# Weight tiles of 4,352 bytes, filler tiles and two moved helpers in a one-core decoder layer: where the operands of TensorE's products start in SBUF

## The chip, the cores and the metric

The kernel runs on one core of a Trainium2 chip, alone, as one program in one launch. The metric is the time of that program on the device in microseconds (us), the median of three runs.

## What is computed

A hybrid decoder layer in float32 for one sequence of 1,024 tokens with 1,024 features: two token mixers side by side (a gated linear recurrence, HGRN2, with four heads, and a forgetting attention, FoX, with eight), merged by gates, then a SwiGLU feed forward of 2,816 hidden features and a gated per-layer input of 256 features.

```
h = rms_norm(x);  z = h @ w_in                       # 1024 -> 5640 columns
y_a = hgrn2(z);   y_b = forgetting_attention(z)
merged = sigmoid(z_a) * (y_a @ w_branch_a) + sigmoid(z_b) * (y_b @ w_branch_b)
x = x + merged @ w_out
hf = rms_norm(x); x = x + (silu(hf @ w_ffn_gate) * (hf @ w_ffn_up)) @ w_ffn_down
hp = rms_norm(x); x = x + sigmoid(hp @ w_ple_gate) * (p @ w_ple_proj)
```

## The kernel before

Everything is kept transposed where it can be, features on the 128 partitions and tokens along the row. A product to float32 accuracy is made of three in the type float32r: each operand is split into a high and a low part, and `mm3` (lines 147 to 151) adds high by high, high by low and low by high in one PSUM bank. In each of these a 128 by 128 piece of weights is the stationary operand (512 bytes on a partition), and half of the tokens, 512 columns of 4 bytes (2,048 bytes on a partition), is the moving operand.

By its loops the program makes 5,688 such products of 512 columns outside the attention's own score and value products:

- the eight products of V for either mixer (`v_products`, lines 239 to 241, where tokens are stationary and weights move): 384;
- projections of z by 128 columns, eight for the heads of HGRN2 and sixteen for the gates: 24 units of 48, that is 1,152;
- branches, output projection and the gate of the per-layer input, 8 units of 48 each: 1,152; the small product with `p`: 96;
- the feed forward's gate and up, 22 tiles of seven half-size blocks (Winograd's form of Strassen's method) with 12 products each: 1,848;
- the way back, lines 1253 to 1256, 44 steps with 24 products each: 1,056.

The attention's score and value products have 287 more with 512 columns. `nproj` (lines 379 to 402) makes six pairs of units with tokens stationary and 256 columns of weights moving: 960 products of 256 columns, and 192 of 264 in the pair that carries the forget gates too.

TensorE's instructions stand in the order in which the code writes them (a manual schedule). The splits are made by ScalarE (`whi`, line 122) and VectorE (`wlo`, line 123) up to two units ahead, from a raw tile that SyncE's queue loads.

What matters for the change is where tiles start in a partition of SBUF. Pools are laid one behind the other: `const`, `xpool`, `wpool` and the later pools `gp`, `xb`, `ap`, `bp`, `dp`, `dq` from the low end, and pools with `side="right"` (`zpool`, `hg`, `fx`, `tp`, `xq`, `op`, `x1p`) from the high end. All sizes in the pools of operands are multiples of 256 bytes but for one: the tiles `raw`, `whi` and `wlo` of `wpool` hold 4 x 264 = 1,056 columns, that is 4,224 bytes or 16.5 times 256. `const` holds small tiles of many sizes.

```
def wide(tag, dt, bufs=None):
    return wpool.tile([P, 4 * 264], dt, tag=tag, bufs=bufs, name=tag)

cm = const.tile([P, 7 * P + 2 * P], U8, name="cm")     # masks of HGRN2
uh = const.tile([16, P], R, tag="uh", name="uh")       # largest scores, two parts
```

So the built program has these starts, as remainders by 256 bytes:

| tiles | start, bytes | remainder |
|---|---|---|
| `xpool`: x, its parts `xhi` and `xlo`, half of the feed forward's operands `xo` | 25,440 + n x 2,048 | 96 |
| `whi`, three buffers | 99,424 / 103,648 / 107,872 | 96 / 224 / 96 |
| `wlo`, three buffers | 112,096 / 116,320 / 120,544 | 224 / 96 / 224 |
| `gp`, `xb`, `ap` (`sahi`, `salo`, `sbhi`, `sblo`), `dp` (`dhi`, `dlo`), `dq` | | 96 |
| right side: `hg`, `fx` (attention), `xq` (ten of the feed forward's operands), `zpool` | | 224 |

The three buffers of `whi` and of `wlo` are taken in turn, so a unit of weights has its high part at 96 and its low part at 224, or the other way round in one unit of three. Slices of 128 or 256 columns are multiples of 256 bytes further on; the slices of 264 columns (1,056 bytes) step by 32 bytes in the remainder.

Of the kernel before, what the change touches and what calls it, by code (L numbers as in the profile page):

```python
# [9 lines left out]
F32 = mybir.dt.float32  # L10
R = mybir.dt.float32r
U8 = mybir.dt.uint8
# [5 lines left out]
DRAM = bass.MemoryType.DRAM  # L18

P = 128  # L20
# [9 lines left out]
NEG = -1.0e30  # L30
LEVELS = (64, 32, 16, 8, 4, 2, 1)
# [3 lines left out]
# weight units, each [128, 1024], in the order in which they are stored  # L35
# [11 lines left out]
# columns of the packed float32 constants  # L47
# [3 lines left out]
# gate tiles made among the products of the mixers: those that go to DRAM (how many before a unit  # L51
# of z, and after all of them), then those that stay on chip
# [8 lines left out]
def layer(ctx, tc, xT, pT, wts, wf_in, consts, masks, outT):  # L61
# [9 lines left out]
    const = ctx.enter_context(tc.tile_pool(name="const", bufs=1))  # L71
    xpool = ctx.enter_context(tc.tile_pool(name="xpool", bufs=32))
# [12 lines left out]
    cm = const.tile([P, 7 * P + 2 * P], U8, name="cm")  # L85
# [10 lines left out]
    def wide(tag, dt, bufs=None):  # L96
        return wpool.tile([P, 4 * 264], dt, tag=tag, bufs=bufs, name=tag)

    def fetch(u):
        if u not in raws:  # L100
            t = wide("raw", F32, 2)
            raws[u] = t[:, 0:D]
            if u in (16, 17):
                # with the columns of the forget gates
                raws[u] = t
                v = t.rearrange("p (k c) -> p k c", c=264)
                dma(v[:, :, 0:256], wts[u].rearrange("p (k c) -> p k c", c=256))
                dma(v[:, :, 256:264],
                    wf_in.rearrange("p (k c) -> p k c", c=8)[:, (u - 16) * 4:(u - 15) * 4])
            else:  # L110
                dma(raws[u], wts[u])
# [35 lines left out]
    def mm3(ps, w, x, k, first, last):  # L147
        """ps += w[k].T @ x[k] to float32 accuracy, from two-part operands"""
        mm(ps, w[0], x[0], start=first, stop=False)  # L149
        mm(ps, w[0], x[1], start=False, stop=False)  # L150
        mm(ps, w[1], x[0], start=False, stop=last)  # L151
# [10 lines left out]
    def split_scaled(src, gain, h):  # L162
        """two float32r parts of src * gain, one half of the tokens"""
        hi = xpool.tile([P, HALF], R, tag="x", name="xhi")
        lo = xpool.tile([P, HALF], R, tag="x", name="xlo")
        act(hi, src, AF.Copy if gain is None else AF.Identity,  # L166
            scale=1.0 if gain is None else gain)
        if gain is None:
            tt(lo, src, hi.bitcast(F32), ALU.subtract)  # L169
        else:  # L170
            stt(lo, src, gain, hi.bitcast(F32), ALU.mult, ALU.subtract)  # L171
        return hi, lo
# [7 lines left out]
    def rms_stats(acc, bank, tag="r8"):  # L180
        """1 / sqrt(mean + eps) over the features, tokens on the partitions"""
        ps = bank()
        for b in range(8):
            mm(ps[:, b:b + 1], acc[:, b * P:(b + 1) * P], ones1, start=True, stop=True)  # L184
        nat = const.tile([P, 8], F32, tag="nat", name="nat")
        r8 = const.tile([P, 8], F32, tag=tag, name="r8")
        nc.vector.tensor_scalar(nat, ps[:, 0:8], 1.0 / D, EPS, ALU.mult, ALU.add)
        ptt(r8, nat, neghalf[:, 0:8], ALU.pow)
        return r8

    def rms_spread(r8, bank):
        """the same on every partition, tokens along the row"""
        rb = const.tile([P, T], F32, tag="rb", name="rb")
        for h in range(2):
            pr = bank()
            broadcast_rows(r8, h, pr)
            nc.scalar.copy(rb[:, h * HALF:(h + 1) * HALF], pr)  # L197
        return rb
# [3 lines left out]
    # ================= input norm, first products =================  # L202
# [8 lines left out]
    w2 = lambda: hg.tile([P, HALF], F32, tag="w2", bufs=NW, name="w2")  # L211

# [3 lines left out]
    def skew(t, off, *dims):  # L216
        """a view of a tile with free dimensions of given steps and sizes"""
        return bass.AP(t.tensor, t.offset + off, [list(t.ap[0])] + [list(d) for d in dims])

    # V of all heads is made in its natural layout, tokens on the partitions. HGRN2 takes its odd  # L220
    # chunks with the tokens in reverse, which makes room for two chunks in one product.
# [73 lines left out]
    # lower bounds of the forget gate: softmax over the two rows of logits  # L295
# [16 lines left out]
    def zproj(u, dst=None):  # L312
        """one 128-column tile of z, transposed: dst[h] = psum * rb; yields between the products"""
        hi, lo = weight(u)
        if dst is None:
            z = zpool.tile([P, T], F32, tag="z", name="z")
            dst = [hv(z, 0), hv(z, 1)]
        else:
            z = None
        for h in range(2):  # L320
            ps = zbank()
            for k in range(KT):
                s = slice(k * P, (k + 1) * P)
                mm3(ps, (hi[:, s], lo[:, s]), hT[h][k], k, k == 0, k == KT - 1)
                run_deferred()
                if k == KT - 1:
                    tt(dst[h], ps, hv(rb, h), ALU.mult)
                yield
        return z

    # a stream of projections that is worked off between the products of the mixers
# [31 lines left out]
    # ================= HGRN2 =================  # L363
    # K and its decays hold the even chunks first, then the odd ones in reverse
# [14 lines left out]
    def nproj(u, n=256):  # L379
        """columns of z with the tokens on the partitions; yields the chunks that are done"""  # L380
# [22 lines left out]
    def hg_project_gate(g):  # L403
        """g of two heads, tokens on the partitions"""
        Gp = [page("G"), page("G")]
        gain.append([t.rearrange("p (c n d) -> p c n d", n=2, d=P) for t in Gp])
        for done in nproj(12 + 2 * g):
            for c, ps in done:
                act(Gp[c // 4][:, c % 4 * 256:c % 4 * 256 + 256], ps, AF.Identity,
                    scale=rx8[:, c:c + 1])  # L410
            yield

    def hg_decay(h, Fp, Qp, b):
        """forget gate, its log summed over each chunk, and silu of q"""
# [4 lines left out]
        # small gates are scaled into the range of Ln  # L419
# [10 lines left out]
        # K = 1 - forget gate, and the summed log in the order of K  # L430
# [16 lines left out]
    def hg_mix(rate, h, K, bK, Fp, Qp, b):  # L447
# [54 lines left out]
        # between the chunks  # L502
# [97 lines left out]
    def fox_gates(fl):  # L600
        """minus the running sum of the log forget gates, eight heads on eight partitions"""
# [25 lines left out]
    def fox_project(g, i, half):  # L627
        """q or k of four heads, normalised, tokens on the partitions"""
# [50 lines left out]
    # the first two tiles of z; the row of 1 / rms is worked out meanwhile  # L679
# [33 lines left out]
    # V of the attention, in two parts  # L713
# [30 lines left out]
    # ================= forgetting attention =================  # L744
# [24 lines left out]
    def fox_norm(pr, i):  # L769
        """the heads in two parts, tokens along the row; the low part replaces the tile"""  # L770
# [13 lines left out]
    def fox_place(pr):  # L784
        """the operands of the score products of two heads"""
# [25 lines left out]
    def fox_mix(pr, steps, before):  # L811
# [3 lines left out]
        # the largest score of each token (its constant cancels in the softmax)  # L815
# [23 lines left out]
        uh = const.tile([16, P], R, tag="uh", name="uh")  # L839
        ul = const.tile([16, P], R, tag="ul", name="ul")  # L840
# [112 lines left out]
    # ================= gates, branches =================  # L953
# [61 lines left out]
    # ================= output projection, residual =================  # L1015
    # The gate and up products of the feed forward are made by Winograd's form of Strassen's
    # method: seven products of half-size blocks for eight. Blocks: tiles k and k + 4 of the
    # features by the two halves of the tokens (b11 and b21 are the first half of the tokens).
# [18 lines left out]
    def split_to(src, gain, hi, lo):  # L1037
        """two float32r parts of src * gain"""
# [66 lines left out]
    # ================= feed forward, hidden features =================  # L1105
# [8 lines left out]
    def ffn_weights(f):  # L1114
        """operands a11 | a12, a22, s1 | s2, s3 | s4 of one tile of gate and up"""
# [9 lines left out]
        # ru becomes s3 | s1 and rg becomes s2 | s4  # L1125
# [11 lines left out]
    def block(n, w, x):  # L1137
        """one product of half-size blocks"""
# [45 lines left out]
    # ================= feed forward, back to the model's features =================  # L1184
# [79 lines left out]
    # ================= per-layer input =================  # L1264
# [22 lines left out]
    # the products of the first two tiles go on while the row of 1 / rms is worked out  # L1287
# [21 lines left out]
def _tiles(w):  # L1309
    """[1024, n * 128] -> one [128, 1024] unit for each 128 columns"""  # L1310
# [67 lines left out]
```

## Time and profile before

| | |
|---|---|
| median of 3 runs | 1682.18 us (1681.9 to 1684.22) |
| span of the profiled execution, first to last instruction | 1680.8 us, 1.4 us under the median |
| TensorE matmuls (PE) | 1657.3 us busy, 99% of the span, 8,218 instructions |
| weight loads (PEld) | 1376.8 us |
| VectorE (DVE) / ScalarE (ACT) / GpSimd (POOL) | 1041.1 / 634.4 / 456.5 us |
| mean granted TensorE clock | 0.998 |
| DMA | 185.94 MB, mean 111 GB/s |

The duration that the trace gives for a matmul (0.39 us for one of 512 columns) reaches from its start to its end through a pipeline in which the next one has long begun. What a matmul costs in a dense stretch is the time from its start to the start of the next, called its **step** from here on: it is read from the column of start times in the timeline.

### The profile page before, as it was taken

What the parts mean: (1) busy time and instruction counts of PE and PEld (TensorE: products, weight loads), DVE (VectorE), ACT (ScalarE), POOL (GpSimd) and SP (SyncE); (2) the same over time, 40 slices, a digit from 0 to 9 for tenths busy, and PEclk for the clock granted to TensorE, in tenths of its full rate; (3) what the DMA queues carried; (4) which work ended last, traced back from release to release, by engine and by line L of the source; (5) the groups of instructions that cost most, each with busy time, mean ns of one, the idle gap of its engine ahead of it and who ended that gap; (6) DMA issues with size and microseconds to landing.
All of it is one profiled execution on the core that took longest, in us unless ns stands there. A gap on an engine that the chain in (4) does not pass through costs nothing. (4 is left out here: it accounts for less than half of the span.)

```text
span 1680.8 us, 21333 instructions
## 1 busy us (share of the span) xinstructions
PE 1657.3 (99%) x8218; PEld 1376.8 (82%) x8218; DVE 1041.1 (62%) x1466; ACT 634.4 (38%) x943; POOL 456.5 (27%) x364
## 2 busy tenths in 40 slices
PE   8999999999999999999999999999999999999998
PEld 6889889999787777778787888888888788788887
DVE  8457677755666686655577776666776542643532
ACT  7244555642423134552334232333233342543310
POOL 2342444431312021122134344344343000200300
PEclk9999999999999999999999999999999999999999
DMA  5323121236264642351433222222221763354011
GB/s 207 100 87 102 63 76 39 76 115 177 90 150 122 174 103 86 128 195 48 150 138 101 75 87 94 83 76 76 76 88 63 245 225 113 119 200 138 33 68 38
DMA packets 93685, 185.94 MB, mean 111 GB/s; under 512 B 11376, under 2 KB 40432, under 8 KB 93584
## 3 DMA queue, kind: packets, MB, share of 16 engines
q1 hardware_dynamic: 93584, 184.59, 33.9%
q8 instruction: 64, 1.05, 0.3%
q14 instruction: 37, 0.30, 0.1%
HBM read 130.95 MB, written 40.96 MB: 102 GB/s over the span
## 5 line engine op out<-in xcount | busy, mean ns | idle before, releaser
L149 PE MATMUL ps_z<-xhi,whi 128*128 128x512 f32 x630 | 256.5, 407 | 0.1
L150 PE MATMUL ps_z<-xlo,whi 128*128 128x512 f32 x630 | 249.5, 396 | 1.1 <-DVE xlo L169 0.9
L151 PE MATMUL ps_z<-xhi,wlo 128*128 128x512 f32 x630 | 249.5, 396 | 0.0
L149 PEld LDWEIGHTS ps_z<-xhi,whi 128*128 128x128 f32 x630 | 120.6, 191 | 24.2 <-ACT xhi L166 1.2
L150 PEld LDWEIGHTS ps_z<-xlo,whi 128*128 128x128 f32 x630 | 119.0, 189 | 25.8 <-DVE xlo L169 2.4
L151 PEld LDWEIGHTS ps_z<-xhi,wlo 128*128 128x128 f32 x630 | 118.5, 188 | 26.1
L122 ACT CAST whi<-raw 128x1024 fp32r<-128x1024 f32 (+1 forms) x69 | 72.2, 1047 | 166.9 <-PE ps_z L150 128.8
L123 DVE TENSOR_TENSOR wlo<-raw,whi 128x1024 fp32r<-128x1024 f32 (+1 forms) x69 | 98.8, 1432 | 34.7 <-ACT whi L122 23.6
L169 DVE TENSOR_TENSOR xlo<-raw,xhi 128x512 fp32r<-128x512 f32 x88 | 58.7, 688 | 92.5 <-ACT xhi L166 85.8
L394 PE MATMUL ps_z<-whi,xhi 128*128 128x256 f32 (+1 forms) x384 | 112.1, 292 | 0.0
L395 PE MATMUL ps_z<-wlo,xhi 128*128 128x256 f32 (+1 forms) x384 | 108.2, 282 | 0.0
L396 PE MATMUL ps_z<-whi,xlo 128*128 128x256 f32 (+1 forms) x384 | 108.0, 281 | 0.0
L882 POOL TENSOR_SCALAR ph<-p 128x512 fp32r<-128x512 f32 (+3 forms) x96 | 53.5, 562 | 170.6 <-ACT p L878 170.2
L1173 POOL TENSOR_TENSOR w<-w,rb 128x512 f32<-128x512 f32 x44 | 62.9, 1429 | 113.7 <-ACT w L1172 113.7
L166 ACT ACTIVATE xhi<-raw 128x512 fp32r<-128x512 f32 x88 | 53.0, 627 | 104.5 <-PE ps_m L150 59.3
L883 DVE TENSOR_TENSOR pl<-p,ph 128x512 fp32r<-128x512 f32 (+3 forms) x96 | 55.9, 590 | 49.5 <-POOL ph L882 49.1
L1199 POOL TENSOR_TENSOR acc<-acc,sq 128x512 f32<-128x512 f32 x14 | 22.2, 1619 | 229.0 <-issue 118.3
L395 PEld LDWEIGHTS ps_z<-wlo,xhi 128*128 128x128 f32 x384 | 72.4, 189 | 0.8 <-DVE wlo L123 0.2
L394 PEld LDWEIGHTS ps_z<-whi,xhi 128*128 128x128 f32 x384 | 72.7, 189 | 0.1
L878 ACT ACTIVATE p<-ps_m 128x512 f32<-128x512 f32 (+3 forms) x96 | 46.1, 491 | 70.5 <-PE ps_m L874 45.8
L1126 POOL TENSOR_TENSOR ru<-ru 128x512 f32<-128x512 f32 x22 | 36.1, 1642 | 133.7 <-DVE wlo L1041 133.7
L396 PEld LDWEIGHTS ps_z<-whi,xlo 128*128 128x128 f32 x384 | 72.3, 188 | 0.0
(465 smaller groups left out, 4394.1 us busy)
## 6 DMA issues: line engine op xcount, KB each, us to landing
raw<-wts SPq DMA_DIRECT2D x71, 512.0 KB
raw<-hid SPq DMA_DIRECT2D x44, 512.0 KB
rg<-wts SPq DMA_DIRECT2D x22, 512.0 KB
ru<-wts SPq DMA_DIRECT2D x22, 512.0 KB
hid<-w SPq DMA_DIRECT2D x44, 256.0 KB
dr<-wts SPq DMA_DIRECT2D x42, 256.0 KB
gd<-gst SPq DMA_DIRECT2D x24, 256.0 KB
g<-gd SPq DMA_DIRECT2D x24, 256.0 KB
```

Of the source, the lines that this page charges most:

```text
L122: nc.scalar.copy(hi, raw)
L123: tt(lo, raw, hi.bitcast(F32), ALU.subtract)
L149: mm(ps, w[0], x[0], start=first, stop=False)
L150: mm(ps, w[0], x[1], start=False, stop=False)
L151: mm(ps, w[1], x[0], start=False, stop=last)
L169: tt(lo, src, hi.bitcast(F32), ALU.subtract)
L394: mm(ps[:, off:off + n], xh[:, cs], hi, start=k == 0, stop=False)
L395: mm(ps[:, off:off + n], xh[:, cs], lo, start=False, stop=False)
L396: mm(ps[:, off:off + n], xl[:, cs], hi, start=False, stop=k == KT - 1)
L882: pts(ph[:, 0:n], p[:, 0:n], 1.0, 0.0, ALU.mult, ALU.add)
L883: tt(pl[:, 0:n], p[:, 0:n], fb(ph[:, 0:n]), ALU.subtract)
L1173: ptt(s, s, hv(rb, h), ALU.mult)
```

## The change

`WIDE` is 17 x 64 = 1,088 columns, so a tile of `wpool` has 4,352 bytes, 17 times 256. A filler tile of 288 bytes in `const` and one of 480 bytes in a new pool on the right side move the ends of those pools to multiples of 256. The masks `cm` (1,152 bytes) leave `const` for the pool of HGRN2, with 12 x 128 = 1,536 bytes, and the two parts of the largest scores, `uh` and `ul` (512 bytes each), leave it for the attention's pool. Comments go too.

```diff
+WIDE = 17 * 64
+PAD = 72
...
     const = ctx.enter_context(tc.tile_pool(name="const", bufs=1))
+
+    const.tile([P, PAD], F32, name="pad")
+    edge = ctx.enter_context(tc.tile_pool(name="edge", bufs=1, side="right"))
+    edge.tile([P, 120], F32, name="edge")
     xpool = ctx.enter_context(tc.tile_pool(name="xpool", bufs=32))
...
-    cm = const.tile([P, 7 * P + 2 * P], U8, name="cm")
...
     def wide(tag, dt, bufs=None):
-        return wpool.tile([P, 4 * 264], dt, tag=tag, bufs=bufs, name=tag)
+        return wpool.tile([P, WIDE], dt, tag=tag, bufs=bufs, name=tag)
...
-                raws[u] = t
-                v = t.rearrange("p (k c) -> p k c", c=264)
+                raws[u] = t[:, 0:4 * 264]
+                v = raws[u].rearrange("p (k c) -> p k c", c=264)
...
+    cm = hg.tile([P, 12 * P], U8, tag="cm", bufs=1, name="cm")
...
-        uh = const.tile([16, P], R, tag="uh", name="uh")
-        ul = const.tile([16, P], R, tag="ul", name="ul")
+        uh = fx.tile([16, P], R, tag="uh", bufs=1, name="uh")
+        ul = fx.tile([16, P], R, tag="ul", bufs=1, name="ul")
```

In the program that is built, every tile of every pool but `const` starts at a multiple of 256 bytes: `xpool` at 23,552, `raw` at 89,088, `whi` at 97,792, `wlo` at 110,848, and so on. What still starts elsewhere is `const` (the identity, 128 before, now 160; small tiles) and three of each four slices of 264 columns. On every engine the instructions are the same and stand in the same order, with the same sizes and the same transfers; the instructions that compute differ in their addresses alone.

## Rows read from the trace of the kernel before

**Rows 1.** The page, parts 1 and 2: span, busy time, granted clock by slice.

```profile
span 1680.8 us, 21333 instructions
PE 1657.3 (99%) x8218; PEld 1376.8 (82%) x8218; DVE 1041.1 (62%) x1466; ACT 634.4 (38%) x943; POOL 456.5 (27%) x364
PEclk9999999999999999999999999999999999999999
```

**Rows 2.** Waits of PE: engine, line waited for, us in total, times, longest.

```profile
PE ps_z L239 <- ACT xhi L166: 5.6, 1, 5.6
PE ps_a L861 <- DVE pl L883: 2.2, 4, 0.8
...
PE ps_z L150 <- DVE xlo L171: 0.2, 1, 0.2
```

**Rows 3.** Timeline of PE at the first products: start us, duration us, what.

```profile
6.59 0.63 PE L241 MATMUL ps_z<-whi,xlo 128*128 128x512 f32 x1
...
7.87 0.63 PE L241 MATMUL ps_z<-whi,xlo 128*128 128x512 f32 x1
```

**Rows 4.** Stretch 6 to 8 us: us, PE busy (x), PEclk, DMA share, GB/s.

```profile
6.00:8.00 2.00, 2.00 (x6) 1.00 1.00 378
```

**Rows 5.** Timeline of PE on the way back: 49 matmuls, first and last.

```profile
1399.63 0.39 PE L151 MATMUL ps_z<-xhi,dlo 128*128 128x512 f32 x1
...
1410.51 0.39 PE L151 MATMUL ps_z<-xhi,dlo 128*128 128x512 f32 x1
```

**Rows 6.** Timeline of PE, per-layer gate: 43 matmuls of a unit, 45 of the next.

```profile
1594.23 0.40 PE L151 MATMUL ps_z<-xhi,wlo 128*128 128x512 f32 x1
...
1604.03 0.39 PE L151 MATMUL ps_z<-xhi,wlo 128*128 128x512 f32 x1
...
1607.67 0.39 PE L149 MATMUL ps_z<-xhi,whi 128*128 128x512 f32 x1
...
1617.84 0.40 PE L151 MATMUL ps_z<-xhi,wlo 128*128 128x512 f32 x1
```

**Rows 7.** Timeline of PE, feed forward: 47 matmuls, first and last.

```profile
999.63 0.40 PE L151 MATMUL ps_m<-xo,sblo 128*128 128x512 f32 x1
...
1010.27 0.39 PE L149 MATMUL ps_m<-xo,sahi 128*128 128x512 f32 x1
```

**Rows 8.** Timeline of PE, feed forward: third triples of two blocks, from 957.72 and 1018.58.

```profile
957.72 0.40 PE L149 MATMUL ps_z<-xo,sbhi 128*128 128x512 f32 x1
...
958.41 0.39 PE L149 MATMUL ps_z<-xo,sbhi 128*128 128x512 f32 x1
...
1017.90 0.39 PE L149 MATMUL ps_z<-xo,sbhi 128*128 128x512 f32 x1
...
1018.58 0.40 PE L149 MATMUL ps_z<-xo,sbhi 128*128 128x512 f32 x1
...
1019.28 0.39 PE L149 MATMUL ps_z<-xo,sbhi 128*128 128x512 f32 x1
```

**Rows 9.** Timeline of PE among the attention's projections: 128x128 products, then 9 matmuls of 256 columns.

```profile
341.38 1.13 PE L495 MATMUL ps_m<-Q,K 128*128 128x128 f32 x8
342.26 0.36 PE L394 MATMUL ps_z<-whi,xhi 128*128 128x256 f32 x1
342.46 0.28 PE L395 MATMUL ps_z<-wlo,xhi 128*128 128x256 f32 x1
...
343.41 0.28 PE L394 MATMUL ps_z<-whi,xhi 128*128 128x256 f32 x1
```

**Rows 10.** Timeline of PE, pair with the forget gates: slices of 264 columns.

```profile
309.01 0.28 PE L394 MATMUL ps_z<-whi,xhi 128*128 128x264 f32 x1
...
310.10 0.28 PE L394 MATMUL ps_z<-whi,xhi 128*128 128x264 f32 x1
310.22 0.28 PE L395 MATMUL ps_z<-wlo,xhi 128*128 128x264 f32 x1
```

## The prediction

> **What bounds the kernel now.** I read the page first, then TensorE's waits, then start times in the timeline. The page shows PE busy for 99% of the span and no slice of its clock row under the top digit, while VectorE, the next engine, stands at 62% [rows 1]. The waits that stop PE are twelve rows that fall from 5.6 us, once at the start, to 0.2 us [rows 2]; no stage is held up by a split or a transfer for long. So the time is the number of products times their step, and the question is what a step is.
>
> A product of 512 columns has a floor that the trace shows. The first products step by (7.87 - 6.59) / 3 = 0.427 us [rows 3], which is 512 columns at 1.2 GHz, the lower level of the clock (the clock column reads 1.00 there all the same [rows 4]); at this pace each column costs one tick and nothing is added, although these operands lie at remainders 96 and 224 too. At 2.4 GHz the same 512 ticks are half of that, 213.3 ns. No dense stretch reaches it:
>
> - On the way back all operands lie at remainder 96. There 48 steps take 10.88 us, 226.7 ns each [rows 5].
> - In the gate of the per-layer input the moving operand lies at 96. The unit with its high part at 224 and its low part at 96 takes 9.80 us for 42 steps, 233.3 ns; the next, with the high part at 96 and the low at 224, 10.17 us for 44 steps, 231.1 ns [rows 6].
> - In the feed forward, where some moving operands lie at 224 (the ten tiles of `xq`) and the weights of three blocks in seven come from the mixed pool, 46 steps take 10.64 us, 231.3 ns [rows 7].
> - Inside its blocks, with weights at 96: three products with the moving operand at 96 take 0.68 us, with it at 224 they take 0.69 us in one block and 0.70 in another [rows 8].
>
> The same instruction, on the same engine at the same clock, thus takes 226.7 to 233.3 ns by where its operands start, and the better place is still 13.4 ns above the floor. TensorE is fed too slowly at the upper clock, and part of that hangs on addresses.
>
> **What the change does to this.** The order of instructions, their sizes and the transfers stay; so nothing is added or taken away on any queue, and no wait changes its place on PE. The filler tiles cost no time. The masks and the largest scores are read and written by the same instructions elsewhere. VectorE, ScalarE and GpSimd get other addresses as well; their work is covered by PE [rows 1], and if a split became somewhat longer or shorter, it would show only in the waits of [rows 2]. The identity keeps a place off the multiples; it only moves in 128-column transposes, whose spacing follows the weight load (below), and I cost it at nothing.
>
> What counts is the step with all operands at remainder 0. No dense product of before has that, so I bound it: 213.3 ns from below (the floor), and 226.7 ns from above (the best place now), as long as 0 is not worse than 96, which is a rival. Between these I take an estimate from the two places that the rows have. A run of 2,048 bytes cut at multiples of 256 begins with a piece of 160 bytes and ends with one of 96 if it starts at 96 (40 and 24 columns), and with 32 and 224 bytes if it starts at 224 (8 and 56 columns). Suppose that a piece shorter than s columns costs s all the same, and that each product loses c besides. At 96 the excess is 32 ticks (226.7 against 213.3): c + (s - 40) + (s - 24) = 32. At 224 it is (0.695 / 3 = 231.7 ns, the mean of the two blocks of [rows 8]) 44 ticks: c + (s - 8) = 44. That gives s = 44 and c = 8. At 0 there are only whole pieces of 64 columns, and c alone is left: 8 ticks, 3.3 ns, a step of 216.7, say **217 ns**. With 0.70 alone the same sum gives c = 16 and 220 ns, so 220 is the upper end of this case. It is a thin model, two unknowns from two readings to 0.01 us, and I keep both bounds for the range.
>
> The Trainium skill (TensorE: Matmul & The Clock Gate, "Wait — 56ns, not 53.3ns?") gives N / 2.4 GHz plus about 2.5 ns for a warm product, 215.8 ns here; by it the sum below would end near 1591. No dense row of this trace shows that figure.
>
> **The sum.**
>
> - Dense products of 512 columns, 5,688 by the loops. Their step now: 1,056 on the way back at 226.7 [rows 5]; 1,848 in the feed forward at 231.3 [rows 7]; the other 2,784 at 231.8 (two units of three at 231.1, one at 233.3 [rows 6]). That is 1,312 us, 230.7 on average. At 217: 13.7 x 5,688 = **77.9 us** less.
> - The attention's own 287 of 512 columns: the same 13.7 ns would be 3.9 us; they wait in a chain through three engines [rows 2], so I take half, **2 us**.
> - 960 products of 256 columns step by (343.41 - 342.46) / 8 = 119 ns [rows 9]. Their floor is not the 106.7 ns of 256 columns but the weight load: eight 128-by-128 passes take 0.88 us, 110 ns each [rows 9]. I take 112: 7 x 960 = 6.7, say **7 us** less; between 0 and 9.
> - 192 products of 264 columns, whose moving slices still start off the multiples in three cases of four: 121 ns now, and those at 0 step no faster (0.12 us at 310.10, against 1.09 / 9 = 0.121 before it [rows 10]). Nothing.
> - New waits. PE's pace rises by 6%, and other engines have to keep it: 62% of VectorE becomes 65%. The rows of waits hold chains that PE just catches (attention's `pl`, the splits of the way back); I add **3 us** for them.
>
> 77.9 + 2 + 7 - 3 = 83.9 us. The profiled execution's span of 1680.8 us is 1.4 below the median; I take the gain from the median: 1682.2 - 83.9 = **1598 us**.
>
> **Rivals.**
>
> *Only the spread goes (0.20).* The excess of 32 ticks at remainder 96 is the cost of loading new weights beside a moving operand whatever the address, and 0 is as good as 96 and no better. For it: those slices of 264 columns that start at 0 are as slow as the rest [rows 10], and in 226.7 ns every step of the way back agrees. Against: in [rows 10] the stationary operand lies at 96 all along, and the weight load is close behind as a limit. Time: 4.0 x 5,688 = 22.8 us plus about 1 us, 1658.
>
> *Half of it goes (0.22).* Short pieces cost less than my model says and c more, so that the step lands between 220 and 225. At 222.5: 8.2 x 5,688 = 46.6 us, with some 4 us elsewhere, 1631.
>
> *Slower (0.05).* With everything at remainder 0, moving operand, weights and the other engines' tiles all begin at the same place of a 256-byte piece, and their reads meet there, always. For it: single steps of 0.22 us occur in [rows 8] where the moving operand and the weights start apart. Against: on the way back both start at 96, and this is the fastest dense stretch. It turns the result if the step passes 230.7 ns; at 238 it adds 7.3 x 5,688 = 41.5 us, 1724.
>
> *No change (0.03).* Addresses don't matter to TensorE, and the differences above are due to the stages. The spread within one stage, between neighbouring units that differ in nothing but buffers [rows 6], is against it. Time 1682. The Trainium skill (SBUF — State Buffer, "Who interferes with whom") says that PE has two independent read ports, one for the moving operand and one for weight loads, and never waits on anyone, by which this rival would hold; the two units of 233.3 and 231.1 ns in [rows 6], and 226.7 in [rows 5], disagree.
>
> **How the numbers follow.** My forecast, a step of 215 to 220 ns, has 0.50; its own range is 1586 to 1620 (213.3 ns, less the 1 to 2 ns that I don't believe can vanish, to 220 ns). With the half (0.22) and the spread alone (0.20) it is 0.92. To leave out no more than 0.2 the range must reach into the spread's case, so it goes to 1660; from below I let it go to 1582, for 214.5 ns with no new wait (16.2 x 5,688 = 92 us, with 2 and 7 more). A measurement of this kernel can tell about 0.2% from no change, 3.4 us: all three of these cases are faster by more, 0.92; no change 0.03; slower 0.05.
>
> **What would show it.** On the way back, start times should be 217 ns apart instead of 226.7, and the two units of the per-layer gate equal to each other and to it. If all stretches stand at 226.7, the spread alone went. The feed forward's third triples should no longer differ from the second. The products of 256 columns should come near 112. PE should stay near 99% busy, with its waits up by a few us; if the step is 217 and the time is over 1615, the waits took the gain, and the list names the engine. A step above 230.7 anywhere in the dense stages makes the prediction wrong altogether.

## The result and the profile after

| | before | changed |
|---|---|---|
| median of the runs compared | 1682.36 us (1681.9 to 1684.22, 4 runs) | 1667.24 us (1666.33 to 1667.54, 4 runs) |
| span of the profiled execution | 1680.8 us | 1665.2 us |

The ratio is 0.9904, with a 95% interval of 0.989 to 0.9918: the change is faster by 0.96%, 15 us, and not by the 84 us that I forecast. The time lies above the top of my range (1660) and 9 us above what my rival "only the spread goes" gave (1658). The direction was right, the size was not, and the direction came out right for another reason than mine, as the experiments show.

The page of the changed kernel, parts 1 and 2, answers to [rows 1]:

```profile
span 1665.2 us, 21335 instructions
PE 1639.5 (98%) x8218; PEld 1375.5 (83%) x8218; DVE 1041.2 (63%) x1466; ACT 634.4 (38%) x943; POOL 455.1 (27%) x364
PEclk9999999999999999999999999999999999999999
```

PE is as full as before, at the same clock. The work of the other engines is what it was to within 1.5 us, so addresses cost or gave them nothing that shows. The list of PE's waits, which answers to [rows 2], has 15 rows in place of 12, with 20.8 us in all in place of 18.2. Its first row is 0.6 us longer:

```profile
PE ps_z L245 <- ACT xhi L171: 6.2, 1, 6.2
```

The timeline of PE on the way back, in the feed forward and in one unit of the per-layer gate (first and last row of each piece) answers to [rows 5, 7, 6]:

```profile
1384.63 0.39 PE L154 MATMUL ps_z<-xhi,dhi 128*128 128x512 f32 x1
...
1395.51 0.39 PE L154 MATMUL ps_z<-xhi,dhi 128*128 128x512 f32 x1
...
984.68 0.39 PE L154 MATMUL ps_m<-xo,whi 128*128 128x512 f32 x1
...
995.56 0.39 PE L154 MATMUL ps_m<-xo,whi 128*128 128x512 f32 x1
...
1579.02 0.39 PE L154 MATMUL ps_z<-xhi,whi 128*128 128x512 f32 x1
...
1589.89 0.39 PE L154 MATMUL ps_a<-ph,hi 128*128 128x512 f32 x1
```

Each piece has 48 steps: 10.88 us on the way back, 10.88 in the feed forward, 10.87 in the unit, that is 226.7, 226.7 and 226.5 ns. The step on the way back, which had every operand at remainder 96 before, has not moved by a nanosecond; the others have come down to it from 231.3 and 231.1 to 233.3. In the trace every single step of the three pieces is 226 or 227 ns, so the products inside a block no longer differ either. This is the picture that the prediction gave for "only the spread goes".

Products of 256 columns, answering to [rows 9]:

```profile
340.85 0.28 PE L401 MATMUL ps_z<-wlo,xhi 128*128 128x256 f32 x1
...
341.93 0.28 PE L401 MATMUL ps_z<-wlo,xhi 128*128 128x256 f32 x1
```

Nine steps take 1.08 us, 120 ns, where I forecast 112 and had read 119 before.

Where the 15.6 us between the two profiled spans lie can be read from the first product of each stage. These rows are the first products of the branches, the feed forward, the way back and the last stage, of the kernel before:

```profile
703.92 0.40 PE L149 MATMUL ps_z<-xhi,whi 128*128 128x512 f32 x1
885.92 0.40 PE L149 MATMUL ps_z<-xo,whi 128*128 128x512 f32 x1
1316.05 0.39 PE L149 MATMUL ps_a<-xhi,whi 128*128 128x512 f32 x1
1561.47 0.39 PE L149 MATMUL ps_a<-ph,hi 128*128 128x512 f32 x1
```

and of the changed kernel:

```profile
701.53 0.39 PE L154 MATMUL ps_z<-xhi,whi 128*128 128x512 f32 x1
879.88 0.39 PE L154 MATMUL ps_z<-xo,whi 128*128 128x512 f32 x1
1302.92 0.39 PE L154 MATMUL ps_a<-xhi,whi 128*128 128x512 f32 x1
1547.64 0.39 PE L154 MATMUL ps_a<-ph,hi 128*128 128x512 f32 x1
```

| stretch | before | changed | difference |
|---|---|---|---|
| start to the branches (projections, both mixers, gates) | 703.9 | 701.5 | -2.4 |
| branches and output projection | 182.0 | 178.4 | -3.6 |
| feed forward | 430.1 | 423.0 | -7.1 |
| way back | 245.4 | 244.7 | -0.7 |
| per-layer input, to the end of the span | 119.3 | 117.6 | -1.8 |

Nearly half of the gain is the feed forward's, and the first stretch, with the mixers and nearly a third of the products of 512 columns, gives a sixth of it.

### The profile page after: what moved, and what is told of

The parts are those of the page before. It is cut to its first block, busy times and chain, and to the rows that moved or that the text cites. A ratio compares the mean times of both kernels' runs of the same rounds, so it can differ in the third digit from the quotient of the medians.

```text
span 1665.2 us, 21335 instructions
## 1 busy us (share of the span) xinstructions
PE 1639.5 (98%) x8218; PEld 1375.5 (83%) x8218; DVE 1041.2 (63%) x1466; ACT 634.4 (38%) x943; POOL 455.1 (27%) x364
## 5 line engine op out<-in xcount | busy, mean ns | idle before, releaser
L156 PE MATMUL ps_z<-xhi,wlo 128*128 128x512 f32 x630 | 246.0, 390 | 0.0
L1134 DVE TENSOR_TENSOR rg<-ru,rg 128x512 f32<-128x512 f32 x22 | 36.7, 1667 | 55.4 <-POOL ru L1133 55.4
```

## The experiments

The spread of the steps had gone and their level had stayed. Two theories could tell why. **Place**: 224 is a bad remainder to start at, 96 and 0 are equally good ones. **Sameness**: what costs is that the two operands of one product start at different remainders, whatever these are. Before, 96 beside 224 was the slow pair and 96 beside 96 the fast one, so the rows shown of the kernel before fit both. The change makes everything good and everything the same at once. My forecast rested on a third, that multiples of 256 are good by themselves, and the way back at 226.7 ns had already spoken against that one.

**e1_all_224: the change without its fillers.** Then the pools of operands all begin at remainder 224.

```diff
-    const.tile([P, PAD], F32, name="pad")
-    edge = ctx.enter_context(tc.tile_pool(name="edge", bufs=1, side="right"))
-    edge.tile([P, 120], F32, name="edge")
```

> The change without its two filler tiles: weight tiles of 4,352 bytes, masks and largest scores moved, but every operand of every pool starts at remainder 224 by 256. Theory 'place' (224 is a bad start, 96 and 0 are good ones): all dense products step by 230 to 234 ns, on the way back too, and the time is 5,688 x 3 to 7 ns over the change, 1685 to 1705 us, no better than before or worse. Rival 'sameness' (what costs is that the operands of one product start at different remainders): all steps 226.7 ns, time 1667 us as with the fillers.

1667.2 us (1667.03 to 1669.16), ratio 0.9908 (0.9893 to 0.9923): the same as the change. A piece of the way back, 48 steps:

```profile
1384.69 0.39 PE L151 MATMUL ps_z<-xhi,dhi 128*128 128x512 f32 x1
...
1395.57 0.39 PE L151 MATMUL ps_z<-xhi,dhi 128*128 128x512 f32 x1
```

10.88 us, 226.7 ns, with every operand at the remainder that "place" calls bad. That theory has fallen, and with it any merit of a start at a multiple of 256. That the filler tiles do nothing for the time here is a coincidence: the moved helpers take 1,152 + 2 x 512 = 2,176 bytes out of `const`, 8.5 times 256, and so the low end goes from 96 to 224 by itself, where the right side lies already.

**e2_weights_96: weight tiles all at 96, right side at 224.**

```diff
-PAD = 72
+PAD = 32
...
-    edge = ctx.enter_context(tc.tile_pool(name="edge", bufs=1, side="right"))
-    edge.tile([P, 120], F32, name="edge")
```

> The weight tiles alone in effect: a filler of 128 bytes puts the low pools at remainder 96 as before, with all weight tiles at 96 now, and the right side stays at 224. Theory 'place': weights by 96, so 226.7 ns in all dense stretches but for products with a moving operand of the right side (in the feed forward about 12 of 84 per tile) and the attention; time 1668 to 1673 us, that is most of the change's gain. Rival 'sameness': the same figure, since low with low now agrees. Rival 'multiples of 256 matter by themselves': little gain, 1675 us or more.

1672.43 us (1672.1 to 1673.38), ratio 0.9938 (0.9922 to 0.9955). Two thirds of the gain come with equal weight tiles while the two ends still differ; the rest needs both ends of SBUF at the same remainder, for the ten operands of the feed forward that lie on the right side. The trace bears this out: the feed forward takes 427.5 us here against 423.0 in the change, 4.4 of the 5.1 us between the two spans. Its dense step is 229.1 ns on average, that of the way back and of the per-layer gate 226.8.

**e3_all_96: both ends at 96.**

```diff
-PAD = 72
+PAD = 32
...
-    edge.tile([P, 120], F32, name="edge")
+    edge.tile([P, 32], F32, name="edge")
```

> Both fillers of 128 bytes: every operand at remainder 96. 'Place' and 'sameness': equal to the change, 1667 us within 2 us, 226.7 ns on every dense stretch. 'Multiples of 256': slower than the change by more than 5 us.

1667.86 us (1665.86 to 1669.05), ratio 0.9908 (0.9893 to 0.9923). Equal to the change again: 0, 96 and 224 are all alike if they are alike everywhere.

**m1_map: all pairs of remainders, by themselves.** A kernel of its own, run once: stretches of 24 products (`RUN`) on a stationary tile `s` and a moving tile `m` that start where I want them, each stretch in another bank than the one before it:

```
def run(s, m, n=512, c=P, k=P):
    ...
    for i in range(RUN):
        mm(ps[0:c, 0:n], s[0:k, i % 4 * P:i % 4 * P + c], m[0:k, i % 2 * 512:i % 2 * 512 + n], start=i == 0, stop=i == RUN - 1)
```

> A kernel of its own that computes nothing of the layer: its output is the input, but for one row block that shows two banks. It runs stretches of 24 products of 512 columns in float32r with the moving operand at one of eight remainders (0 to 224 by 32) and the stationary one at one of eight, 64 stretches; then fewer columns, fewer weight columns (96, 64, 32), fewer rows, bfloat16, and mixed starts. 'Place': a row and a column of the table stand out (224, and perhaps 160 and 192), the others are 226.7 ns. 'Sameness': the diagonal is fast, the rest is slow. If the 32 ticks above the floor are the weight load beside the stream, they shrink with 96, 64 and 32 weight columns (24, 16, 8 ticks: 223, 220, 217 ns) and stay 32 ticks with fewer moving columns (120 ns at 256); if they are a share of the stream (17/16), 64 weight columns still give 226.7 ns and 256 columns 113 ns. bfloat16 shows whether 4-byte elements are the cause: 213 to 216 ns if they are, 226.7 if not.

The timeline merges a stretch into one row, so the difference of two starts divided by 24 gives its step. In the names a, b, c to h stand for remainders 0, 32, 64 to 224:

```profile
22.36 5.62 PE L50 MATMUL psc<-mva,sta 128*128 128x512 f32 x24
27.82 5.75 PE L50 MATMUL psd<-mva,stb 128*128 128x512 f32 x24
33.41 5.76 PE L50 MATMUL pse<-mva,stc 128*128 128x512 f32 x24
...
66.92 5.77 PE L50 MATMUL psc<-mvb,sta 128*128 128x512 f32 x24
72.52 5.64 PE L50 MATMUL psd<-mvb,stb 128*128 128x512 f32 x24
78.00 5.75 PE L50 MATMUL pse<-mvb,stc 128*128 128x512 f32 x24
```

Moving and stationary at the same remainder: 5.46 and 5.48 us; apart: 5.59 and 5.60. The mean step of each of the 64 stretches without its first two products, in ns, in three rows of the table:

| moving at | stationary 0 | 32 | 64 | 96 | 128 | 160 | 192 | 224 |
|---|---|---|---|---|---|---|---|---|
| 0 | 226.7 | 233.4 | 233.5 | 234.3 | 233.6 | 233.3 | 228.9 | 233.2 |
| 96 | 233.3 | 228.9 | 233.2 | 226.7 | 233.4 | 233.4 | 234.3 | 233.5 |
| 224 | 232.9 | 233.4 | 234.3 | 233.5 | 233.3 | 228.9 | 233.2 | 226.7 |

The diagonal is fast in all eight rows. To within some 1 ns the rows are one row shifted: only the **distance** counts, the start of the moving operand less that of the stationary one, taken by 256 bytes. At distance 0 the step is 226.7 ns, with the moving operand 64 ahead 228.9, at the six others 232 to 234. The same map puts the remaining excess over 213.3 ns, 32 ticks of the 2.4 GHz clock, to a test. The first three of these stretches have fewer weight columns (96, 64, 32) and so less of a weight load, the fourth has 96 rows in place of 128:

```profile
399.52 5.71 PE L50 MATMUL psa<-mva,sta 128*96 128x512 f32 x24
405.07 5.69 PE L50 MATMUL psb<-mva,sta 128*64 128x512 f32 x24
410.60 5.73 PE L50 MATMUL psc<-mva,sta 128*32 128x512 f32 x24
416.17 5.61 PE L50 MATMUL psd<-mva,sta 96*128 96x512 f32 x24
```

5.55, 5.53 and 5.57 us, 230 to 232 ns: at this distance a quarter of the weight columns does not shorten the step, it lengthens it by some ns. So the 32 ticks do not follow the amount of weights that is read beside the stream, as the rival "only the spread goes" had it. With 96 rows the step settles at 226.7 too. Nor are the ticks a sixteenth of the stream: at distance 0, 256 columns settle at 120.0 ns and 320 at 146.7, 13.3 ns above their own 106.7 and 133.3, where a sixteenth would give 113.3 and 141.7. And bfloat16, 512 columns, settles at 216 ns.

**e5_apart_128: put the operands apart again.**

```diff
+    gap = ctx.enter_context(tc.tile_pool(name="gap", bufs=1))
+    gap.tile([P, 32], F32, name="gap")
     wpool = ctx.enter_context(tc.tile_pool(name="wpool", bufs=3))
```

> The changed kernel with a filler of 128 bytes between the pool of x and the pool of weights: x at remainder 0, weights and what lies behind them at 128, the right side at 0. All starts are still multiples of 128. 'Sameness': about 4,750 of the 5,688 dense products (projections, V, branches, way back, per-layer gate, three quarters of the feed forward) have moving and stationary operand 128 apart and step by 233.3 ns instead of 226.7: 31 us over the change, 1695 to 1702 us, slower than the kernel before; the output projection stays at 226.7. 'Place': no start is at 224 or 96, so 1667 us.

1689.51 us (1687.89 to 1691.28), ratio 1.0041 (1.0027 to 1.0055): with 128 bytes of filler the changed kernel becomes slower than the one before, 22 us over the change where I expected 31. A piece of the way back (x at 0, weights at 128; 47 steps) and one of the output projection (both at 128; 48 steps):

```profile
1414.60 0.41 PE L157 MATMUL ps_a<-xlo,dhi 128*128 128x512 f32 x1
...
1425.52 0.39 PE L156 MATMUL ps_a<-xhi,dhi 128*128 128x512 f32 x1
...
829.64 0.39 PE L158 MATMUL ps_z<-mh,wlo 128*128 128x512 f32 x1
...
840.52 0.39 PE L158 MATMUL ps_z<-mh,wlo 128*128 128x512 f32 x1
```

232.3 ns and 226.7. By "place" the time would have been 1667 us. So the distance sets the step in the layer itself; the price of distance is 5 to 6 ns there rather than the map's 6.9, and why it is smaller was not tested.

**m2_fine: finer distances, other numbers of columns.** Nearly the same `run`, with the moving operand `o` columns further on; run once.

> A kernel of its own again, whose output is the input but for one row block. Distances between the starts of the moving and the stationary operand in finer steps (4 to 28 bytes, both ways), and in steps of 32 bytes for 256, 264, 384 and 448 columns; then weights that alternate between two starts, a moving operand read backwards or with a step, weights with a step. If sameness has to be exact, a distance of 4 bytes already gives 233 ns at 512 columns; if it is about 32-byte or 64-byte pieces, small distances stay near 226.7. If the lock between the two streams is what sets the step, other numbers of columns have their best distance elsewhere, and some distance gives less than the 120 ns that 256 columns take at distance 0 (down to the 110 ns of a weight load); if 32 ticks are fixed for 4-byte elements, 256 columns take 117 to 120 ns at every distance.

At 512 columns a distance of 4 bytes gives 236.7 ns, 8 bytes 231.7, 20 bytes 240.0, 28 bytes 230.0: sameness has to be exact, and none of the distances tried beats 0. At 256 columns it is otherwise. Distances 0, 32 and so on to 224:

```profile
110.86 3.02 PE L50 MATMUL psc<-mva,sta 128*128 128x256 f32 x24
113.72 3.00 PE L50 MATMUL psd<-mva,sta 128*128 128x256 f32 x24
...
127.92 2.89 PE L50 MATMUL psa<-mva,sta 128*128 128x256 f32 x24
130.64 3.00 PE L50 MATMUL psb<-mva,sta 128*128 128x256 f32 x24
```

At distance 0 the step settles at 120.0 ns, among the slowest of these eight, and at 192 it is 2.72 / 24 = 113.3. So 256 columns have their own best distance. That fits the change having made them slower, and points to a better version.

The same kernel tells more of whose distance counts. In one stretch of 512 columns the weights alternate: two products on weights at the moving operand's remainder (`sta`), the third on weights 128 bytes off (`ste`), eight times over:

```profile
269.53 0.62 PE L68 MATMUL psa<-mva,sta 128*128 128x512 f32 x2
269.99 0.40 PE L68 MATMUL psa<-mva,ste 128*128 128x512 f32 x1
...
275.08 0.63 PE L68 MATMUL psb<-mva,sta 128*128 128x512 f32 x2
```

Eight threes take 5.55 us, 694 ns each. If a product's own two operands were all that counts, it would be 2 x 226.7 + 233.6 = 687. By the starts of the single products the three steps are 226.6, 232.7 and 234.0 ns: the product ahead of the one with the distant weights is slow as well, though its own operands start alike. In the kernel before, the second unit of [rows 6] shows the same three on average: 226.7, 232.7 and 234.0 ns. There the trace has the load of a product's weights beside the product ahead of it:

```profile
1607.90 0.40 PE L150 MATMUL ps_z<-xlo,whi 128*128 128x512 f32 x1
1607.90 0.19 PEld L151 LDWEIGHTS ps_z<-xhi,wlo 128*128 128x128 f32 x1
```

So a unit with one of its two parts apart does not lose in the products on that part alone: with the low part apart two products of three are slow (231.1 ns on average), with the high part apart all three (233.3). That the loss arises while these weights are loaded fits this, but was not shown.

**e6_shift_192 and e7_fillers_alone.** The first shifts the split weights of ten units of 256-column products by 48 columns in their tiles:

```diff
-            hi, lo = [wide(t, R)[:, 0:raw.shape[1]] for t in ("whi", "wlo")]
+            o = 48 if u in (12, 13, 14, 15, 18, 19, 20, 21, 22, 23) else 0
+            hi, lo = [wide(t, R)[:, o:o + raw.shape[1]] for t in ("whi", "wlo")]
```

> The changed kernel, with the split weights of ten of the twelve units that move 256 columns (all but the pair with the forget gates) laid 48 columns, 192 bytes, into their tiles; tokens, stationary there, stay at remainder 0. The map gave 113.3 ns for 256 columns at a distance of 192 bytes and 120.0 at 0. Theory 'lock' (the distance by 256 between the two operands of a product sets the step, with another best distance for 256 columns): 960 products at 113 to 114 instead of 120 ns, 5 to 6.5 us less than the change, 1661 to 1662 us. Rival 'only equal starts are good': no better or some us worse, 1667 to 1670 us. If groups of six to twelve products are too short for the lock: 1665 to 1667 us.

1665.1 us (1664.72 to 1665.22), ratio 0.9895 (0.9881 to 0.991), 2 us under the change's median, a third of what the theory "lock" gave, and within the last case of the expectation. The products of 256 columns step by 113 to 114 ns in some groups and by 117 to 118 in others, as here:

```profile
338.65 0.28 PE L401 MATMUL ps_z<-whi,xhi 128*128 128x256 f32 x1
...
340.30 0.28 PE L403 MATMUL ps_z<-whi,xlo 128*128 128x256 f32 x1
```

14 steps in 1.65 us are 118 ns. Over all of them the average is 116.5 ns, against 119.6 in the change, which makes 2.8 us on the 900 steps counted.

The second goes back to the old weight tiles and keeps the fillers:

```diff
-WIDE = 17 * 64
+WIDE = 4 * 264
```

> The changed kernel with the weight tiles of before (4,224 bytes): fillers and moved helpers alone. Everything lies at remainder 0 but every second buffer of the weight pool, at 128. 'Sameness': the dense products from those buffers stay apart as before, so only the feed forward's products with the ten right-side tiles and the attention gain: 3 to 6 us of the 15, 1677 to 1680 us. Rival 'the fillers do it': 1667 to 1670 us.

1680.79 us (1679.47 to 1681.65), ratio 0.9988 (0.9978 to 0.9997): 1.7 us, less than I expected. Without equal tiles the fillers give little: the feed forward is 2.7 us shorter in the trace (427.4 us), and no other stretch gains. Equal tiles with the two ends apart (e2) give 10.6 us, equal tiles with equal ends 15: only together do all the feed forward's products lie the same.

**m3_groups: bfloat16 at ten distances, and short groups of 256 columns.**

> A kernel of its own, output as in the other maps. First bfloat16, 512 columns, at ten distances between moving and stationary operand (0 to 224 bytes by 256): if the lock belongs to 4-byte streams, all step by 216 ns; if not, the distances differ by some ns. Then, at eight distances, four groups each of twelve float32r products of 256 columns in the layer's pattern (high by high, high by low, low by high), each group behind four float32 products of 128 columns, as in the layer: 'lock with a settling time': at distance 192 the first products of a group take 117 to 120 ns and the later ones 113; at distance 0 all come to 120 within a few products. If a group of twelve is too short, 192 shows no figure under 116 ns, and the 2.1 us that the shift by 192 brought in the layer have another source.

bfloat16 at distances 0, 4 and 16 bytes (the other seven are like the last two):

```profile
21.33 5.35 PE L56 MATMUL psc<-bx,bw 128*128 128x512 bf16 x24
26.52 5.34 PE L56 MATMUL psd<-bx,bw 128*128 128x512 bf16 x24
31.70 5.34 PE L56 MATMUL pse<-bx,bw 128*128 128x512 bf16 x24
```

5.18 us for 24, 215.8 ns at every distance: products of bfloat16, with 2 bytes an element, do not show the effect. Of the four groups at distance 192 the first steps by 113.3 ns, the other three by 117.7, from the fourth product to the end of the group. These rows are a stretch of the first group and a stretch of the second:

```profile
144.74 0.28 PE L73 MATMUL psg<-mva,sta 128*128 128x256 f32 x1
...
145.65 0.28 PE L73 MATMUL psg<-mva,sti 128*128 128x256 f32 x1
...
147.01 0.28 PE L73 MATMUL psa<-mva,sta 128*128 128x256 f32 x1
...
147.95 0.28 PE L73 MATMUL psa<-mva,sti 128*128 128x256 f32 x1
```

Eight steps take 0.91 us there and 0.94 here. The group falls into one of two rhythms and stays in it; what chooses between them I did not find. The groups are not alike in everything: each reads weights 512 bytes further on in their tiles and writes another bank, and at distance 64 too the first of the four was the fast one, so the choice may hang on these. It is not a settling time, as I had thought. It would explain why the shift in the layer brings a part only.

**e8_change_again and e9_shift_again.** The change and the shift on one chip.

> The changed kernel again, beside the next run on the same chip: 1667 us.

> The kernel of e6_shift_192 again, on the chip on which the change runs too: if the shift by 192 bytes is worth the 2.7 us that its 256-column products are shorter, 1664.5 to 1665.5 us, 2 us under the change; if the 2.1 us were another chip's, the same as the change within 0.5 us.

1666.64 us (1665.92 to 1668.71) for the change and 1663.87 us (1663.67 to 1664.81) for the shift; their runs do not overlap. The intervals of their ratios to the kernel before, 0.9905 (0.989 to 0.9919) and 0.9886 (0.9869 to 0.9902), do. The shifted version is the best that I have, 2 to 3 us under the change.

## Why the prediction was wrong

**What bounds the kernel: right.** PE is full before and after, the clock is the same, and the listed waits grew by 2.6 us only: the step is the time.

**"A step of 217 ns at remainder 0": wrong, and the cause of nearly all of the miss.** The model of short pieces (s = 44, c = 8) was fitted to two readings. It took remainder 0 for a better place than 96 because a run that starts there has no broken piece. The step at remainder 0 is 226.7 ns, as it is at 96 (e3) and at 224 (e1): the remainder means nothing by itself, and m1_map shows that the distance between the two operands does. The change is faster because it makes the starts equal, not because it makes them multiples of 256; that the direction came out as forecast is luck. In that light [rows 5] were already the best case, not a middling one. The sign was there to be read: [rows 8] put 0.69 and 0.70 us on products whose moving operand alone had gone to 224, and the same loss appeared when the weights alone had. Two different operands with the same loss at 224 and no loss at 96, where their partners lay, is what sameness looks like. I had both ends of SBUF at different remainders in front of me and read the difference as a property of one of them. The 0.69 and the 0.70 us, from which the prediction took a mean and an upper end of 220 ns, are both 0.696 in the trace. The term of 77.9 us, with the 2 us for the attention's own products, was worth 17.5 by the start times of all products of 512 columns; the attention's own share in it is 0.1 us (233.1 ns before, 232.5 after, on average over steps under 260 ns).

**"Only the spread goes": the right case, with a chance of 0.20, and too large.** I priced it at 22.8 + 1 us on 512 columns; it measured 17.5. That 0 is as good as 96 and no better was right. That the excess is the cost of loading weights whatever the address was not: the distance changes it, and fewer weight columns do not shorten it. The stages account for the difference in size. The feed forward gave 7.1 us where my 231.3 ns, from one row group, made it 1,848 x 4.6 = 8.5: over the whole stage the step before was 230.6. The mixers with their 1,536 dense products gave some 5 us on these where 231.8 ns made it 7.8: the products of V came down to 226.7 ns but had started from 230.6, and the projections only went from 232.0 to 228.6 (averages of the steps under 260 ns). The projections stand in short runs between other products; that this keeps them above 226.7 was not tested.

**"Products of 256 columns come to 112": wrong in sign.** Over all of them they went from 118.0 to 119.6 ns, and cost 1.4 us instead of giving 7. (The 119 that I read in [rows 9] comes of two rounded starts; the eight steps take 0.943 us, 118 ns.) I took the weight load's 110 ns as the floor that they would fall to, and m2_fine shows that distance 0, best for 512 columns, is among the worst for 256.

**"Nothing for 264 columns", "no cost on other engines", "moved helpers free": right.** The first by a poor reason: in [rows 10] the partner of a moving operand at 0 stayed at 96, so these rows could not show what equal starts do. The products of 264 columns went from 121.7 to 121.0 ns. m2_fine has 120.0 for them at distance 0 and 120 to 123 at seven others, so there was little to gain.

**"3 us of new waits": about right in size, not in its reason.** The listed waits rose by 2.6 us, and e1, e3 and e8 have 20.3 to 20.8 us of them too. But I had the term from a pace that rises by 6%, and it rose by 1%; 0.6 us of it are the later start of the first product in this execution.

**The Trainium skill's figures.** The 215.8 ns that the Trainium skill gives for a warm product (TensorE: Matmul & The Clock Gate, "Wait — 56ns, not 53.3ns?") is what bfloat16 takes here (215.8); float32r stays at 226.7 at best. And the Trainium skill's statement that PE's two read ports are independent (SBUF — State Buffer, "Who interferes with whom") does not hold for the time here: with float32r operands the distance between what the two read changes the step by 3% (226.7 to 233.6 ns).

## What to carry to other kernels

When one instruction has two durations and the addresses differ, compare pairs before places: ask what the two operands have to each other, and try the remedy at another absolute address before fitting a price to one. Here, for products of 512 columns, it is enough that tiles of float32r operands have sizes that are whole multiples of 256 bytes and that pools at either end of SBUF begin at the same remainder; which one is indifferent. A steady stretch that is already fast may be the bound itself: no stage of 512 columns came below the 226.7 ns that the way back had from the start.

## What the runs showed of the hardware

- With float32r operands, the step of a dense 512-column product depends on the distance between the starts of the moving and the stationary operand, taken by 256 bytes: 226.7 ns at 0, 228.9 at 64, 230 to 240 at the other distances tried, down to 4 bytes. The remainder that the two share made no difference (0, 96 and 224 in the layer, eight of them in m1_map).
- The next product's weights count too: a product whose own operands start alike takes 232.7 ns when the weights of the one behind it lie 128 bytes off (m2_fine, and the kernel before).
- The best of the distances tried depends on the number of columns: 0 for 512, 192 for 256 (113.3 ns against 120.0 at distance 0).
- bfloat16 shows none of it, 215.8 ns at ten distances; and at the lower clock, in the first products of a run, float32r takes 427 ns at distance 0 and 224 alike. So the excess of about 32 ticks at distance 0 was seen with float32r at the upper clock alone. It does not shrink with fewer weight columns (230 to 232 ns with 96, 64 and 32). What it is in the machine was not found.
- Products of 256 columns keep a rhythm. Groups of twelve at the same distance step by 113.3 or by 117.7 ns from the fourth product on; the groups differ in the slice of weights and in the bank.
